# Residual-stream norms: squares summed on GpSimd, the last one by TensorE, with a later due time for that sum

## The chip, the cores and the metric

One core of one Trainium2 chip. The metric is the device time of one execution in microseconds, the median of several runs. The engines are TensorE (PE in the profile, its weight loads PEld), VectorE (DVE), ScalarE (ACT), GpSimd (POOL) and SyncE (SP), which here only issues DMAs.

## The reference, cut to what matters

Two layers over 1024 tokens of width 1024, batch 1. Each layer is a mixer (layer 0: RG-LRU and gated DeltaNet; layer 1: HGRN2 and RWKV-7), a SwiGLU feed-forward part, and a gated embedding add. Each of the three starts from a normed residual stream:

```
def _rms_norm(x, w):
    y = x * rsqrt(mean(x * x, axis=-1) + 1e-6)
    return y * w

hn = _rms_norm(h, norm_mix[layer]);  h = h + mixer(hn)
h = h + _swiglu(_rms_norm(h, norm_ffn[layer]), w_gate, w_up, w_down)
h = h + sigmoid(_rms_norm(h, norm_ple[layer]) @ ple_w_gate) * (p[layer] @ ple_w_up)
return _rms_norm(h, norm_final)
```

## The kernel before, in words

The stream is kept transposed: a half of the sequence (512 tokens) is eight tiles `h[0]` to `h[7]` of 128 channels by 512 tokens, float32. Every product with a weight matrix is made from three matmuls per 128 x 128 block, on operands split in a high and a low part (`hi*hi`, `hi*lo`, `lo*hi`): `whi`, `wlo` of the weights, `xhi`, `xlo` of the normed stream. One output tile of a width-1024 product is 24 such matmuls into one PSUM tile `acc`, of which there are four; the mixers use four others, `mx`.

The order of work is: input projection of both halves of layer 0; then four blocks, each of `project_out` (the mixer's output added to `h`), `ffn` and `ple`; behind the two blocks of layer 0 stands the input projection of layer 1 for that half (`odd_in`, through `project_in`). The mixers run beside these stages.

The norm's factor depends on the token alone, so the products are made from `h` times the norm's weight, without the factor, and the factor `rs` is multiplied in when a product leaves PSUM. `norm_scale` (from line 1154) makes `rs`. It squares the eight tiles on ScalarE (line 191 by the helper `act`) into tiles `tmp` (five buffers), adds them up pair after pair on VectorE (line 170 by `add`, seven adds), sums over the 128 channels with one float32 matmul whose weights are ones (line 196 by `mm`, into an `acc` tile; at the very first call into an `mx` tile), and then takes the inverse root: a `ts` on VectorE (line 187), Ln and Exp on ScalarE, three VectorE steps (`newton`). It is called 11 times: once for the first input projection, four times in `ffn`, four times in `ple`, twice in `odd_in`. The profile shows each float32 128x512 matmul as two instructions.

Every instruction gets a due time, `tc.cur_priority`, set by `at`; a planner with a cost model of its own plays the program through when it is built, and on each engine takes, of what is ready, the one with the smallest due time. The order it finds is then fixed. `self.clock` counts 216 for each matmul of a product (`PASS`). A product's matmuls are due at `clock`; after each output tile `products` (line 1239) sets `at(self.clock - EVAC)`, 45000 earlier, so what takes a result out of PSUM goes ahead of nearly everything. `norm_scale` is called just there: in `ffn` (line 1302) after both first tiles (gate and up, 48 matmuls) are written down, in `ple` (line 1350) after the first tile, in `project_in` (line 1271) after two tiles. Its squares, its adds, its matmul and its inverse root all carry that early due time. The splitting of weights (`weights`, line 1224) is due at `clock - WSPLIT`, 40000 ahead of its product. The mixers' instructions have due times that `spread` lays evenly over the stages beside which they run.

GpSimd is given only fills and masks: memsets and affine selects.

Of the kernel before, what the change touches and what calls it, by code (L numbers as in the profile page):

```python
# [15 lines left out]
ALU = mybir.AluOpType  # L16
# [3 lines left out]
P = 128  # L20
D = 1024
KD = D // P
# [8 lines left out]
PASS, START = 216, 100000  # L31
FETCH, WSPLIT = 28700, 40000
SPLIT, EARLY = 12000, 60000
EVAC = 45000
# [76 lines left out]
class Trunk:  # L111
# [1039 lines left out]
        for k in range(KD):  # L1151
            self.load(d[k], self.h[k])

    def norm_scale(self, acc_tile=None):

        acc = self.tmp()
        self.act(acc, self.h[0], AF.Square)
        for k in range(1, KD):
            s = self.tmp()
            self.act(s, self.h[k], AF.Square)  # L1160
            self.add(acc, acc, s)
        ps = (acc_tile or self.acc)()
        self.mm(ps, self.ones.broadcast_to([P, P]), acc)
        x = self.tmp()
        y = self.dense.tile([P, HALF], F32, tag="rs", bufs=1, name=self.name("rs"))
        self.ts(x, ps, 1.0 / D, 1e-6, ALU.mult, ALU.add)
        self.rsqrt(x, y, acc)
        return y
# [125 lines left out]
    def ffn(self, ops, wg, wu, wd, side=None):  # L1294
        starts = FSTARTS
        cols = [[self.products(w, 0, KD, P * k0, P * nk, ops) for w in (wg, wu)] for k0, nk in zip(starts, FCHUNKS)]
        rs = None

        def hidden(c):
            nonlocal rs  # L1300
            g, up = (next(p) for p in cols[c])
            if rs is None:
                rs = self.norm_scale()
            gs, t = self.tmp(), self.tmp()
            self.mul(gs, g, rs)
            self.act(t, gs, AF.Tanh, scale=0.5)
            self.stt(t, t, 1.0, gs, ALU.add, ALU.mult)
            self.mul(t, t, up)
            self.mul(t, t, rs)
            op = self.operand("g")  # L1310
            self.split(t, *op)
            return op


        ahead = []
        for c, (k0, nk) in enumerate(zip(starts, FCHUNKS)):
            hid = ahead + [hidden(c) for _ in range(nk - len(ahead))]
            ahead = [hidden(c + 1)] if c + 1 < len(FCHUNKS) else []
            for m, ps in enumerate(self.products(wd, k0, nk, 0, D, hid)):
                self.stt(self.h[m], ps, 0.5, self.h[m], ALU.mult, ALU.add)  # L1320
            if side is not None:
                next(side, None)
# [24 lines left out]
    def ple(self, ops, layer, up):  # L1347
        rs = None
        for m, g in enumerate(self.products(self.w["ple_w_gate"][layer], 0, KD, 0, D, ops)):
            if rs is None:  # L1350
                rs = self.norm_scale()
            t, u = self.tmp(), self.tmp()
            self.load(u, up[m])
            self.mul(t, g, rs)
            self.act(t, t, AF.Tanh, scale=0.5)
            self.stt(t, t, 1.0, u, ALU.add, ALU.mult)
            self.stt(self.h[m], t, 0.5, self.h[m], ALU.mult, ALU.add)
# [169 lines left out]
```

## Time and profile before

| | |
|---|---|
| median of 3 runs | 2938.49 us (2933.05 to 2941.14) |
| profiled execution, its own time | 2940.61 us |
| its span, first to last instruction | 2938.9 us |
| PE busy | 2870.5 us, 98% |
| DVE busy | 1956.7 us, 67% |
| ACT busy | 1255.6 us, 43% |
| POOL busy | 26.6 us, 1% |
| mean granted clock of TensorE | 0.99 |

How to read it: busy is the time in which an engine had an instruction of its own under way. Matmuls are pipelined: a product's matmul is shown with 0.39 us, but in a row of them one starts every 0.23 us, so what a matmul costs is read from starts, not from durations. An idle stretch is put down to whatever signalled last before the engine went on.

### The profile page before, as it was taken

The page shows a single profiled execution, that of the slowest core. Times are in us where ns is not written, and L with a number is a line of the kernel's source. Part 1 is how long each engine was busy: PE and PEld are TensorE (multiplying, and loading weights), DVE is VectorE, ACT ScalarE, POOL GpSimd, SP SyncE. Part 2 cuts the span into 40 slices and gives each one's busy share as a digit, 9 for nine tenths or more (in the row PEclk, how much of TensorE's full clock was granted, in tenths as well). Part 3 has the DMA queues.
Part 4 walks back from the last instruction along what each step waited for, and adds up shares of the span by engine and source line. Part 5 has one row for each costly group of instructions (what it writes and reads, how often), then busy time and mean ns, then how long its engine had stood idle before and what let it go on. Part 6 is the DMA issues. An engine that isn't in the chain of part 4 may idle for free.

```text
span 2938.9 us, 38745 instructions
## 1 busy us (share of the span) xinstructions
PE 2870.5 (98%) x15102; PEld 2338.9 (80%) x15102; DVE 1956.7 (67%) x3313; ACT 1255.6 (43%) x1784; POOL 26.6 (1%) x97
## 2 busy tenths in 40 slices
PE   8999999999999999999999999999999999999997
PEld 7888878878878877878877788777877777888886
DVE  7576666746686557837787674784887586655457
ACT  5354653333254636234444533533552554422234
POOL 1000000000000000000000000000000000000000
PEclk9999999999999999999999999999999999999998
DMA  6453652333345553423333544532334234343333
GB/s 207 147 171 123 215 183 89 110 83 108 87 120 175 159 180 114 107 74 100 91 106 106 162 133 146 156 97 70 101 112 109 72 111 140 96 127 93 101 89 105
DMA packets 197287, 357.79 MB, mean 122 GB/s; under 512 B 64848, under 2 KB 100816, under 8 KB 197104
## 3 DMA queue, kind: packets, MB, share of 16 engines
q1 hardware_dynamic: 197104, 355.33, 39.6%
q8 instruction: 118, 1.93, 0.3%
q14 instruction: 65, 0.53, 0.1%
HBM read 298.61 MB, written 56.66 MB: 121 GB/s over the span
## 4 chain that ended last, share of the span: by engine, by line
PE 84%; DVE 9%; ACT 3%; issue 2%; DMA 2%; SPq 0%; DVEq 0%; ACTq 0%
PE acc L196 72%; PE mx L196 11%; DVE wlo L170 2%; DVE w L183 2%; DVE w L170 1%; DVE tmp L170 1%; PE mx L207 1%; ACT w L191 1%; ACT whi L339 1%; DVE cols L170 1%; ACT L191 0%; DMA zin<-z_k 0%; DMA tmp<-mixed 0%; DVE tmp L183 0%; SPq L210 0%
## 5 line engine op out<-in xcount | busy, mean ns | idle before, releaser
L196 PE MATMUL acc<-xhi,whi 128*128 128x512 f32 x2832 | 1126.0, 398 | 14.3 <-ACT whi L339 9.1
L196 PE MATMUL acc<-xlo,whi 128*128 128x512 f32 x2832 | 1117.1, 395 | 2.2 <-DVE xlo L170 2.1
L196 PE MATMUL acc<-xhi,wlo 128*128 128x512 f32 x2832 | 1112.5, 393 | 2.8 <-DVE wlo L170 2.7
L339 ACT CAST whi<-wraw 128x1024 fp32r<-128x1024 f32 (+1 forms) x450 | 463.4, 1030 | 1142.5 <-PE acc L196 837.6
L196 PEld LDWEIGHTS acc<-xhi,whi 128*128 128x128 f32 x2832 | 532.5, 188 | 132.3 <-ACT whi L339 10.5
L196 PEld LDWEIGHTS acc<-xlo,whi 128*128 128x128 f32 x2832 | 533.2, 188 | 120.5 <-DVE xlo L170 7.6
L196 PEld LDWEIGHTS acc<-xhi,wlo 128*128 128x128 f32 x2832 | 532.8, 188 | 120.4 <-DVE wlo L170 5.7
L170 DVE TENSOR_TENSOR wlo<-wraw,whi 128x1024 fp32r<-128x1024 f32 (+1 forms) x450 | 538.6, 1197 | 77.3 <-ACT whi L339 74.8
L170 DVE TENSOR_TENSOR tmp<-acc,rs 128x512 f32<-128x512 f32 (+1 forms) x205 | 140.7, 689 | 344.4 <-PE acc L196 340.5
L196 PE MATMUL acc<-ghi,whi 128*128 128x512 f32 x736 | 290.2, 395 | 1.0 <-ACT ghi L339 1.0
L196 PE MATMUL acc<-ghi,wlo 128*128 128x512 f32 x736 | 287.6, 391 | 0.0
L196 PE MATMUL acc<-glo,whi 128*128 128x512 f32 x736 | 287.5, 391 | 0.0
L170 DVE TENSOR_TENSOR tmp<-tmp,acc 128x512 f32<-128x512 f32 x88 | 60.3, 685 | 160.3 <-PE acc L196 160.0
L191 ACT ACTIVATE w<-w 128x1024 f32<-128x1024 f32 (+2 forms) x124 | 113.3, 920 | 117.3 <-DVE w L170 52.8
L196 PEld LDWEIGHTS acc<-ghi,whi 128*128 128x128 f32 x736 | 138.0, 188 | 30.7 <-ACT ghi L339 1.9
L196 PEld LDWEIGHTS acc<-ghi,wlo 128*128 128x128 f32 x736 | 138.2, 188 | 29.2 <-issue 0.3
L196 PEld LDWEIGHTS acc<-glo,whi 128*128 128x128 f32 x736 | 138.3, 188 | 28.5 <-DVE glo L170 0.6
L183 DVE SCALAR_TENSOR_TENSOR h<-acc,h 128x512 f32<-128x512 f32 x144 | 98.5, 685 | 58.2 <-PE acc L196 57.3
L191 ACT ACT_TABLE_LOAD x85 | 109.1, 1283 | 9.6 <-DVE w L187 4.1
L183 DVE SCALAR_TENSOR_TENSOR w<-zin,cols,w 128x256 f32<-128x256 f32 x192 | 83.0, 478 | 9.7 <-ACT w L191 9.4
L191 ACT ACTIVATE tmp<-tmp 128x512 f32<-128x512 f32 x120 | 75.6, 630 | 31.7 <-DVE tmp L170 30.8
L183 DVE SCALAR_TENSOR_TENSOR tmp<-tmp,tmp 128x512 f32<-128x512 f32 x120 | 82.1, 685 | 9.6 <-ACT tmp L191 9.1
(300 smaller groups left out, 2534.2 us busy)
## 6 DMA issues: line engine op xcount, KB each, us to landing
wraw<-in_ffn_w_gate_dram SPq DMA_DIRECT2D x88, 512.0 KB, 3.6
wraw<-in_ffn_w_up_dram SPq DMA_DIRECT2D x88, 512.0 KB, 3.6
wraw<-in_ffn_w_down_dram SPq DMA_DIRECT2D x64, 512.0 KB, 3.6
wraw<-in_o_w_in_dram SPq DMA_DIRECT2D x60, 512.0 KB, 3.6
wraw<-in_e_w_in_dram SPq DMA_DIRECT2D x48, 512.0 KB, 3.7
wraw<-in_ple_w_gate_dram SPq DMA_DIRECT2D x32, 512.0 KB, 3.6
wraw<-in_ffn_w_down_dram SPq DMA_DIRECT2D x32, 384.0 KB, 3.0
up<-tmp SPq DMA_DIRECT2D x32, 256.0 KB, 2.9
```

Of the source, the lines that this page charges most:

```text
L170: (eng or self.nc.vector).tensor_tensor(out, a, b, op=op)
L183: self.nc.vector.scalar_tensor_tensor(out, a, s, b, op0=op0, op1=op1)
L191: self.nc.scalar.activation(out, a, f, **kw)
L196: self.nc.tensor.matmul(out, lhsT, rhs, start=start, stop=stop)
L207: self.nc.tensor.transpose(out, a, self.ident)
L339: self.nc.scalar.copy(hi, src)
```

## The change: what it does

In all calls of `norm_scale`, the first six of the seven adds go to GpSimd. The seventh is left out: the ones-matmul is run twice into the same PSUM tile, over the sum of the first seven squares and then over the eighth square alone.

In `ffn` and `ple`, the two ones-matmuls and what follows them in `norm_scale` get a later due time: the `clock` at which the second output tile's matmuls of that stage are due (in `ffn` that is `clock - 24 * PASS`, since the clock already stands behind two tiles). Behind `norm_scale` the due time is set back to what it was. The calls in `project_in` pass no `when` and keep the early due time.

```diff
-    def norm_scale(self, acc_tile=None):
+    def norm_scale(self, acc_tile=None, when=None):
         acc = self.tmp()
         self.act(acc, self.h[0], AF.Square)
         for k in range(1, KD):
             s = self.tmp()
             self.act(s, self.h[k], AF.Square)
-            self.add(acc, acc, s)
+            if k < KD - 1:
+                self.tt(acc, acc, s, ALU.add, self.nc.gpsimd)
         ps = (acc_tile or self.acc)()
-        self.mm(ps, self.ones.broadcast_to([P, P]), acc)
+        if when is not None:
+            self.at(when)
+        for i, t in enumerate((acc, s)):
+            self.mm(ps, self.ones.broadcast_to([P, P]), t, i == 0, i == 1)
...
             if rs is None:      # ffn
-                rs = self.norm_scale()
+                rs = self.norm_scale(when=self.clock - 24 * PASS)
+                self.at(self.clock - EVAC)
...
             if rs is None:      # ple
-                rs = self.norm_scale()
+                rs = self.norm_scale(when=self.clock)
+                self.at(self.clock - EVAC)
```

## Rows read from the trace of the kernel before

**Rows 1.** The page, part 1: busy us (share) x instructions, by engine.
```profile
PE 2870.5 (98%) x15102; PEld 2338.9 (80%) x15102; DVE 1956.7 (67%) x3313; ACT 1255.6 (43%) x1784; POOL 26.6 (1%) x97
```
**Rows 2.** The page, part 4: the chain that ended last, shares by engine.
```profile
PE 84%; DVE 9%; ACT 3%; issue 2%; DMA 2%; SPq 0%; DVEq 0%; ACTq 0%
```
**Rows 3.** Waits of PE: who waited for whom, us in total, times, longest.
```profile
PE mx L196 <- DVE keepC L183: 4.9, 4, 2.7
PE acc L196 <- DVE tmp L170: 4.7, 2, 3.7
PE mx L207 <- DVE keepB L170: 3.0, 2, 2.7
...
PE mx L196 <- DVE tmp L170: 1.4, 1, 1.4
```
**Rows 4.** Timeline of PE around the ones-matmul of the first `ffn`: start, us, instruction.
```profile
460.00 1.02 PE L196 MATMUL acc<-tmp,ones 128*128 128x512 f32 x2
460.45 0.79 PE L196 MATMUL acc<-xlo,whi 128*128 128x512 f32 x1
461.08 0.39 PE L196 MATMUL acc<-xhi,wlo 128*128 128x512 f32 x1
461.31 0.40 PE L196 MATMUL acc<-xhi,whi 128*128 128x512 f32 x1
```
**Rows 5.** Groups by line and shape: count, busy us, mean ns, idle before.
```profile
L170 DVE TENSOR_TENSOR tmp<-tmp,tmp 128x512 f32<-128x512 f32 x77 | 52.8, 685 | 2.5 <-ACT tmp L191 2.3
...
L196 PE MATMUL acc<-tmp,ones 128*128 128x512 f32 x20 | 11.5, 657 | 4.7 <-DVE tmp L170 4.7
```
**Rows 6.** Groups of POOL by line and shape.
```profile
L287 POOL TENSOR_SCALAR_AFFINE_SELECT lm<-lm 128x128 f32<-128x128 f32 x6 | 2.8, 471 | 0.3
L526 POOL MEMSET cols<- 128x512 f32 x4 | 2.1, 530 | 253.9 <-PE mx L196 240.3 <-DMA h<-in_x_dram 13.6
```
**Rows 7.** Timeline of DVE, 16.7 to 19.5 us.
```profile
16.73 0.68 DVE L170 TENSOR_TENSOR tmp<-tmp,tmp 128x512 f32<-128x512 f32 x1
...
17.52 0.78 DVE L170 TENSOR_TENSOR tmp<-tmp,tmp 128x512 f32<-128x512 f32 x1
```
**Rows 8.** Timeline of POOL, 16.7 to 19.8 us.
```profile
17.91 0.66 POOL L287 TENSOR_SCALAR_AFFINE_SELECT lm<-lm 128x128 f32<-128x128 f32 x1
...
19.40 0.34 POOL L287 TENSOR_SCALAR_AFFINE_SELECT lm<-lm 128x128 f32<-128x128 f32 x1
```
**Rows 9.** Timeline of PE at the third `ple`, 2398.8 to 2409 us.
```profile
2403.63 2.07 PE L196 MATMUL acc<-tmp,ones 128*128 128x512 f32 x2 [3.71 <-DVE tmp L170]
2404.72 1.42 PE L196 MATMUL acc<-xhi,whi 128*128 128x512 f32 x1
2408.85 0.44 PE L207 MATMUL mx<-ident,keepB 128*128 128x128 f32 x1 [2.71 <-DVE keepB L170]
```
**Rows 10.** Timeline of DVE in the same stretch.
```profile
2402.90 0.68 DVE L170 TENSOR_TENSOR tmp<-tmp,tmp 128x512 f32<-128x512 f32 x1
2403.50 1.22 DVE L170 TENSOR_TENSOR w<-keepA 128x1024 f32<-128x1024 f32 x1
2405.74 0.69 DVE L187 TENSOR_SCALAR tmp<-acc 128x512 f32<-128x512 f32 x1 [1.03 <-PE acc L196]
...
2407.48 1.22 DVE L170 TENSOR_TENSOR keepB<-keepB,w 128x1024 f32<-128x1024 f32 x1
```
**Rows 11.** Windows: us, busy (x) by engine, granted clock, DMA share, GB/s.
```profile
2402.60:2412.80 10.20, 6.45 (x19) 4.53 (x20) 9.17 (x13) 6.06 (x7) 0.00 (x0) 0.50 0.40 128
```
**Rows 12.** Timeline of PE at the fourth `ple`.
```profile
2876.86 1.12 PE L196 MATMUL acc<-tmp,ones 128*128 128x512 f32 x2 [1.00 <-DVE tmp L170]
```
**Rows 13.** Timeline of PE at the first input projection.
```profile
22.01 1.12 PE L196 MATMUL mx<-tmp,ones 128*128 128x512 f32 x2 [1.37 <-DVE tmp L170]
```
**Rows 14.** Timeline of DVE at the first `odd_in`, 919 to 940 us.
```profile
920.67 0.69 DVE L170 TENSOR_TENSOR tmp<-tmp,tmp 128x512 f32<-128x512 f32 x1
...
926.99 0.68 DVE L170 TENSOR_TENSOR tmp<-tmp,tmp 128x512 f32<-128x512 f32 x1
...
936.79 0.69 DVE L183 SCALAR_TENSOR_TENSOR rs<-tmp,rs 128x512 f32<-128x512 f32 x1
937.51 1.94 DVE L170 TENSOR_TENSOR tmp<-acc,rs 128x512 f32<-128x512 f32 x3
```

## The prediction

> **What bounds the kernel now.** I read the busy shares first. PE is busy 98% of the span, DVE 67%, POOL 1% [rows 1], and the chain that ended last lies on PE for 84% [rows 2]. So time is gained or lost where PE stands still, or where it is given more or less work. Second, the waits of PE: they are short, and many different things end them. What concerns this change is two waits for the last add of a norm, 4.7 us in `acc` sums, and one of 1.4 us in the first sum [rows 3]. That is 6.1 us on three of the eleven calls; on the other eight PE did not stand still for the sum at all. Third, the timelines around the three. They show that one of them costs more than its idle time.
>
> **The added matmul.** Each call gets a second ones-matmul. Its price is read from starts: the first of its two instructions starts at 460.00, the next product's matmuls at 460.45 and 461.08, the one after at 461.31 [rows 4]. From 460.00 to 461.08 PE did the ones-matmul and one matmul of the product; an undisturbed one takes 0.23 us (461.08 to 461.31). So 1.08 - 0.23 = 0.85 us for one ones-matmul. The 657 ns that the groups give for each of its two instructions [rows 5] are pipelined durations and would overstate it. Eleven calls: 11 x 0.85 = +9.4 us. It has no cover: PE is the bound, the operands are full-size, and only idle time just behind it could hide it, which in eight calls isn't there. At half clock one costs about twice that, so the bounds are 9.4 and 19; I take +9.4, since nearly all calls fall in stretches at full clock.
>
> **The third `ple` (2403 us).** PE waits 3.71 us for the last add, runs one sum and one product matmul, and waits 2.71 us for the mixer's `keepB` [rows 9]. In between the granted clock is 0.50, that is 1.2 GHz, for 10.2 us after the idle [rows 11], in which PE was busy 6.45 us; at full clock that would have been half. So this place loses 3.71 + 2.71 + 3.2 = 9.6 us. The cause is DVE, which has a queue without gaps here, the norm's adds in it, and then itself waits 1.03 us for the sum that PE could not start, with `keepB` behind that [rows 10]. The change takes seven adds of 0.60 us (start to start, 2402.90 to 2403.50) out of this queue, 4.2 us, and the 1.03 us as well. `keepB` then ends 5.2 us earlier, and PE goes on at 2403.6 in place of 2408.85. The sum that was already done by then comes later, 0.85 us. Net -4.4 us. What is late next is `keepB` again, so PE still stands for some 3.7 us and the clock probably still falls; if not, all 9.6 us go. On the other side, if POOL's adds hold DVE up (below), DVE is no earlier and the place is up to 3 us worse. I take -4.4, from the rows of this very place; bounds -9.6 and +3.
>
> **The fourth `ple` (2877 us).** PE waits 1.00 us for the last add [rows 12] in the middle of the stage's first tile. Planned behind that tile, some 5 us later, the sum finds its squares ready. -1.0 us; bounds -1.0 and 0.
>
> **The adds on POOL.** The trace shows no two-input instruction on POOL. The nearest rows: a fill of the same 128x512 takes 0.53 us, an affine select of a quarter of the size 0.47 us [rows 6], which scales to 1.9. I take 1.2 us, the middle, between 0.53 and 1.9. In `ffn` and `ple` the squares come 2 to 5 us apart, as the tiles of `h` do, the eighth square passes POOL by, and the sum is due a tile later: the adds are hidden there whichever bound holds. In `odd_in` they are not spread out: the seven adds on DVE start from 920.67 to 926.99 [rows 14]; six on POOL at 1.2 us take 7.2 us, about the same, at 1.9 us 11.4 us, 4 us late. The early due time stays there, so PE may wait; the planner knows some POOL price and will place the sum by it. I take +0.3 us for each of the two calls, bounds 0 and 4. In the first input projection the chain is similar, with the mask building in POOL's queue between the adds; the wait of 1.37 us [rows 13] may vanish or grow by 2. I take +0.5.
>
> **DVE's relief, and its port.** DVE loses 77 adds of 0.60 us, 46 us in all. Off the path this is worth nothing. Against it: when a POOL select ran beside an add of DVE, the add took 0.78 us in place of 0.68 [rows 7] and the select 0.66 in place of 0.34 [rows 8]. So the two engines slow each other here, and 66 adds of 1.2 us could cost DVE up to 79 us, more than it is relieved of. The Trainium skill (SBUF — State Buffer, "Who interferes with whom") says that a VectorE instruction with two SBUF inputs contends with a GpSimd instruction that reads SBUF, the later one being fully blocked. By that rule DVE gains nothing and the 2403 us place gets no better; it is the second rival, and the stretch at 17.5 us agrees with it in kind, though 0.10 us there is far from a full block.
>
> **The later due time.** `rs` itself is due some 40 us later too, so the ts, Ln, Exp and the three Newton steps now stand behind weight splits (1.2 us each) and mixer work on DVE. Before, `rs` was finished 9 to 10 us after its last add (926.99 to 936.79) and products left PSUM from 937.51 on [rows 14]. The cover is the four `acc` tiles: the sum's tile is free after the ts, so PE can fill three more tiles, 3 x 24 x 0.23 = 16 us of products and more with mixer work between, before it needs the first one back. A chain of 8 to 14 us fits. I take 0; if it took over 20 us, PE would stop in each such stage.
>
> **The sum.** +9.4 - 4.4 - 1.0 + 0.6 + 0.5 = +5.1 us. The profiled execution took 2940.61 us itself (span 2938.9 and 1.7 around it), so 2945.7 for it; it lies 2.1 us above the median of 2938.49, and for a median I forecast 2943.5 us, 0.17% slower. About 0.3% (8.8 us) is what a measurement of this kernel can tell from no change, so this counts as the same. The planner will also reorder other work, the mixers' above all, whose waits make most of PE's idle time; I put that at 0 with some 8 us either way.
>
> **The rivals.**
> *1, faster: the relief of DVE reaches further.* Then the whole 9.6 us at 2403 us go, and other waits of PE for DVE shrink: `keepC` 4.9, `keepB` 3.0 [rows 3], each of which brings a stretch at half clock like that in [rows 11]. For it: DVE is what PE waits for at most places. Against it: the adds stand only near norms, and just one of the long waits does. Price, with these 7.9 us and some 6 for the half clock behind them: 9.4 - 9.6 - 1.0 - 14 = -15 us, 2923 us. It decides if DVE's queue is what is late in the last 10 us before other waits too.
> *2, slower: POOL's adds block DVE.* Each of the 66 adds holds DVE by its own length; then 2403 us is 3 us worse, and each of the other ten calls costs PE about 1 us. 9.4 + 3 + 10 = +22, less the 1.0: about 2959 us. It decides if DVE instructions beside a POOL add are seen at 1.2 us or more above their usual time.
> *3, slower: `rs` comes too late for the PSUM tiles.* In `ffn` and `ple` the chain behind the sum exceeds 20 us, and PE stops for some 2 us in each of eight stages, with the clock falling behind it: 5 + 16 = +21, 2959 us. For it: due times of splits go ahead of it. Against it: 16 us of cover and more.
> *4, the change does not do what it says:* the planner puts the sums where they were, in the first tile. Then the 1.0 and part of the 4.4 stay lost: +9, 2947 us, still near the bound.
>
> **Chances.** Forecast, with 4 in it: 0.53; rival 1: 0.21; rival 2: 0.14; rival 3: 0.08; other reordering to the slower side: 0.04. Range for 8 in 10: 2925 to 2959, from nearly rival 1 to rivals 2 and 3; the forecast's own is 2935 to 2951. Faster by over 0.3%: 0.21. Within: 0.52. Slower by over 0.3%: 0.27, rivals 2 and 3, the rest, and a hundredth from case 4.
>
> **What would show it.** PE has 22 more matmul records (15124) and DVE 77 instructions fewer; POOL's busy time rises by 35 to 125 us. In the waits of PE, none for `tmp` at the third and fourth `ple`. The ones-matmuls lie behind the first 24 matmuls of each `ffn` and `ple`, four records in a row, 1.7 us from the first to the next product matmul but one. At the third `ple`, PE's idle is 3 to 4 us in place of 6.4. The forecast is wrong if PE's idle time as a whole (span less busy time, 68 us [rows 1]) moves by more than 8 us, or if DVE's two-input instructions get longer beside POOL's adds.

## The result, and the profile after

The changed kernel takes 2969.2 us (median of 4 runs, 2967.35 to 2970.36), the kernel before 2938.4. The ratio is 1.0107, 95% interval 1.0095 to 1.0119: slower by 1.07%. The forecast was 2943.5 us in a range of 2925 to 2959, so it missed by 26 us, and the time lies 10 us above the range. The profiled executions that are compared below took 2967.4 and 2940.6 us.

First the busy shares, part 1 of the page of the changed kernel, against [rows 1]:

```profile
PE 2884.1 (97%) x15124; PEld 2342.4 (79%) x15124; DVE 1943.1 (66%) x3236; ACT 1254.7 (42%) x1782; POOL 129.8 (4%) x163
```

The counts are as the diff has them: 22 more matmul records, 77 DVE instructions fewer, 66 more on POOL. PE is busy 13.6 us longer, but the span grew by 26.7 us (2938.9 to 2965.6): half of the loss is PE standing still. And DVE, relieved of 77 adds that were 52.8 us in [rows 5], lost only 13.6 us of busy time, so its other instructions got longer.

The waits of PE in the changed kernel (who waited for whom, us in total, times, longest), against [rows 3]:

```profile
PE acc L196 <- POOL tmp L170: 5.3, 2, 3.6
PE mx L196 <- POOL tmp L170: 5.0, 1, 5.0
...
PE acc L196 <- DVE xlo L183: 3.1, 3, 2.0
```

The waits for DVE's last add are gone, and 10.3 us of waits for POOL's are there in their place.

Where the time was lost can be read without guessing, because both kernels run the same 10704 product matmuls in almost the same order. I set the start of the n-th of them in one trace against its start in the other. The difference grows in few places:

```
place                             difference, before -> behind it    step, us
first input projection             0.7 ->  8.8                       +8.2
first ple (layer 0)                8.2 ->  9.7                       +1.4
first odd_in                       9.7 -> 19.0                       +9.3
second ple (layer 0)              17.1 -> 23.1                       +6.0
second odd_in                     23.1 -> 29.3                       +6.1
just ahead of the third ple       29.0 -> 30.4                       +1.4
third ple (layer 1)               30.4 -> 25.6                       -4.8
fourth ple (layer 1)              25.8 -> 26.8                       +1.0
each of the four ffn                                                 +0.9 to +1.0
```

The sum over everything is +26.8 us; the steps listed come to some 32. Steps of 2 to 3 us also come from the length of half-clock stretches at places where nothing changed, so a single step is good to about that. The trace of before has many of these: 60.5 us at half clock in all, where the changed kernel has 63.3, and where e9 below, which keeps the order of PE and DVE and the time of before, has 38.4.

**The three sums of the input projections.** At the first one (timeline of PE, start, us, instruction, idle before):

```profile
18.71 0.50 PE L196 MATMUL acc<-xhi,wlo 128*128 128x512 f32 x1 [1.33 <-DVE wlo L170]
...
19.98 0.40 PE L196 MATMUL acc<-xlo,whi 128*128 128x512 f32 x1
25.33 3.78 PE L196 MATMUL mx<-tmp,ones 128*128 128x512 f32 x4 [4.96 <-POOL tmp L170]
28.12 1.42 PE L196 MATMUL acc<-xhi,wlo 128*128 128x512 f32 x1
```

PE stands for 4.96 us, in place of the 1.37 of [rows 13], and before that for 1.33 us because DVE's `wlo` is late, a wait that the runs with the adds on DVE do not have here. Besides, the sum now stands behind 32 product matmuls in PE's fixed order, where it stood behind 42 before: the planner took POOL's chain of six adds to be done 10 x 0.23 = 2.3 us sooner than DVE's of seven. POOL's timeline in that stretch shows why it was not:

```profile
13.83 3.39 POOL L170 TENSOR_TENSOR tmp<-tmp,tmp 128x512 f32<-128x512 f32 x2 [8.00 <-ACT tmp L191]
...
17.67 1.56 POOL L285 TENSOR_SCALAR_AFFINE_SELECT lm<-lm 128x128 f32<-128x128 f32 x2
19.18 0.70 POOL L287 TENSOR_SCALAR_AFFINE_SELECT lm<-lm 128x128 f32<-128x128 f32 x2
19.84 2.62 POOL L170 TENSOR_TENSOR tmp<-tmp,tmp 128x512 f32<-128x512 f32 x2
...
24.01 1.26 POOL L170 TENSOR_TENSOR tmp<-tmp,tmp 128x512 f32<-128x512 f32 x1
```

The first two adds take 3.39 us together, the others 1.3 us each, and the mask building of POOL's old work is queued between the second and the third add, from 17.2 to 19.8. At the first `odd_in` there is nothing else in the queue, and it is the chain alone. PE, then POOL, then DVE in the changed kernel:

```profile
935.57 0.50 PE L196 MATMUL acc<-xlo,whi 128*128 128x512 f32 x1 [0.73 <-DVE xlo L183]
939.71 3.78 PE L196 MATMUL acc<-tmp,ones 128*128 128x512 f32 x4 [3.64 <-POOL tmp L170]
```

```profile
930.07 9.58 POOL L170 TENSOR_TENSOR tmp<-tmp,tmp 128x512 f32<-128x512 f32 x6 [58.99 <-ACT tmp L191]
```

```profile
930.62 1.52 DVE L183 SCALAR_TENSOR_TENSOR h<-tmp,h 128x512 f32<-128x512 f32 x1
932.06 0.59 DVE L183 SCALAR_TENSOR_TENSOR w<-mx,cnbe,vb 128x128 f32<-128x128 f32 x2
932.58 2.93 DVE L183 SCALAR_TENSOR_TENSOR xlo<-h,cols,xhi 128x512 fp32r<-128x512 f32 x2
936.75 1.78 DVE L183 SCALAR_TENSOR_TENSOR xlo<-h,cols,xhi 128x512 fp32r<-128x512 f32 x1 [1.24 <-ACT xhi L191]
```

Six adds take 9.58 us, 1.6 each, where DVE's seven took 7.0 between its other work [rows 14]. And DVE's `xlo`, 0.74 us before, now takes 1.2 to 1.8 us. The two small matrix instructions `w<-mx,...`, which read PSUM and one SBUF tile, keep their 0.34. After the idle comes the half clock, granted clock 0.50, the lower of TensorE's two levels (us, busy by engine, granted clock, DMA share, GB/s):

```profile
23.50:30.30 6.80, 4.97 (x8) 2.62 (x9) 2.73 (x7) 1.44 (x3) 3.02 (x10) 0.50 0.19 40
938.30:945.10 6.80, 5.39 (x9) 2.94 (x10) 0.92 (x2) 0.30 (x1) 2.98 (x6) 0.50 0.15 48
1603.90:1614.10 10.20, 10.20 (x87) 7.86 (x87) 5.80 (x7) 5.13 (x8) 2.53 (x2) 0.50 0.43 123
```

Half of PE's busy time in such a stretch is lost. So the 9.3 us of the first `odd_in` are 4.8 of idle (3.64, 0.73 and a smaller one), 5.39 / 2 = 2.7 of half clock, and 0.85 for the second sum, 8.4 in all; 0.9 us stays open. At the second `odd_in` PE does not wait for POOL at all. It waits for `xlo`:

```profile
1690.45 0.50 PE L196 MATMUL acc<-xlo,whi 128*128 128x512 f32 x1 [2.00 <-DVE xlo L183]
```

With 0.69 us for the mixer's `r_S` right behind it, the idle there is 2.7 us.

**The second `ple`.** No sum is late here; DVE, then POOL, then PE:

```profile
1597.47 3.08 DVE L183 SCALAR_TENSOR_TENSOR xlo<-h,cols,xhi 128x512 fp32r<-128x512 f32 x2
1600.48 0.68 DVE L183 SCALAR_TENSOR_TENSOR h<-acc,h 128x512 f32<-128x512 f32 x1
1601.19 1.24 DVE L621 STREAM_TRANSPOSE m<-m 32x1024 f32<-32x1024 f32 x1
```

```profile
1596.97 1.29 POOL L170 TENSOR_TENSOR tmp<-tmp,tmp 128x512 f32<-128x512 f32 x1 [236.72 <-ACT tmp L191]
1598.72 1.29 POOL L170 TENSOR_TENSOR tmp<-tmp,tmp 128x512 f32<-128x512 f32 x1 [0.46 <-ACT tmp L191]
```

```profile
1602.57 0.18 PE L196 MATMUL mx<-m,pm 32*32 32x32 f32 x1 [1.57 <-DVE m L621]
```

Two `xlo` took 3.08 us beside two POOL adds, where two take some 1.4 without. The second ended at 1600.55 us, 0.54 us behind the end of the second POOL add at 1600.01. It is so throughout: 22 `xlo` of the changed kernel began while a POOL add had more than 0.2 us still to run, and every one ended 0.55 us behind the end of that add. The two engines do not share the time, one waits for the other. The mixer's transpose behind them came 1.57 us late for PE, and the third window above, 10.2 us at half clock, followed. This is POOL's work slowing DVE, with nobody waiting for POOL.

**The added sums and the third `ple`.** Around the first `ffn`, against [rows 4]:

```profile
467.94 1.02 PE L196 MATMUL acc<-tmp,ones 128*128 128x512 f32 x2
468.40 0.79 PE L196 MATMUL acc<-xhi,wlo 128*128 128x512 f32 x1
469.02 1.02 PE L196 MATMUL acc<-tmp,ones 128*128 128x512 f32 x2
469.48 0.79 PE L196 MATMUL acc<-xhi,whi 128*128 128x512 f32 x1
```

From 467.94 to 469.02 PE did one sum and one product matmul, 1.08 us: the price of a sum is 0.85 us again. At the third `ple`, against [rows 9]:

```profile
2429.66 0.39 PE L196 MATMUL acc<-xhi,whi 128*128 128x512 f32 x1
2431.73 1.12 PE L196 MATMUL acc<-tmp,ones 128*128 128x512 f32 x2 [1.68 <-POOL tmp L170]
2432.29 0.80 PE L196 MATMUL acc<-xlo,whi 128*128 128x512 f32 x1
```

The idle is 1.68 us in place of 6.4, and at 0.39 to 0.40 us a matmul the clock did not fall. But the sum stands behind one matmul of the stage's first tile, as before, not behind the tile. And 12 us ahead of it PE waits 1.20 us for the mixer's `w` on DVE, which it did not in the trace of before: the step just ahead of the third `ple`. With it the place gains 3.3 us, not 4.8. The same two steps stand in e1, e7 and e10, three of the other runs with these POOL adds.

### The profile page after: what moved, and what is told of

The parts are those of the page before. It is cut to its first block, busy times and chain, and to the rows that moved or that the text cites. A ratio compares the mean times of both kernels' runs of the same rounds, so it can differ in the third digit from the quotient of the medians.

```text
span 2965.6 us, 38868 instructions
## 1 busy us (share of the span) xinstructions
PE 2884.1 (97%) x15124; PEld 2342.4 (79%) x15124; DVE 1943.1 (66%) x3236; ACT 1254.7 (42%) x1782; POOL 129.8 (4%) x163
## 5 line engine op out<-in xcount | busy, mean ns | idle before, releaser
L196 PE MATMUL acc<-xhi,whi 128*128 128x512 f32 x2832 | 1125.9, 398 | 14.9 <-ACT whi L339 10.3
L170 DVE TENSOR_TENSOR wlo<-wraw,whi 128x1024 fp32r<-128x1024 f32 (+1 forms) x450 | 540.1, 1200 | 83.2 <-ACT whi L339 80.6
L170 POOL TENSOR_TENSOR tmp<-tmp,tmp 128x512 f32<-128x512 f32 x66 | 103.7, 1571 | 1439.1 <-ACT tmp L191 1438.1
L183 DVE SCALAR_TENSOR_TENSOR h<-acc,h 128x512 f32<-128x512 f32 x144 | 98.5, 685 | 61.2 <-PE acc L196 60.5
```

Source lines behind the costliest of these rows:

```text
L170: (eng or self.nc.vector).tensor_tensor(out, a, b, op=op)
L183: self.nc.vector.scalar_tensor_tensor(out, a, s, b, op0=op0, op1=op1)
L196: self.nc.tensor.matmul(out, lhsT, rhs, start=start, stop=stop)
```

## The experiments

Four things could cost: waits for POOL's chain at the three sums with the early due time (A), the added sums (B), POOL's adds slowing DVE (C), and the later due time. Each run was timed beside the kernel before.

| run | median, us | ratio to before, 95% interval |
|---|---|---|
| the change | 2969.2 | 1.0107 (1.0095 to 1.0119) |
| e1, input projections as before | 2946.9 | 1.0032 (1.0021 to 1.0043) |
| e2, the adds on DVE | 2943.7 | 1.0025 (1.0016 to 1.0034) |
| e3, one sum | 2967.0 | 1.0098 (1.0082 to 1.0113) |
| e4, the due time alone | 2938.3 | 1.0005 (0.9996 to 1.0015) |
| e5, later due time in the projections too | 2962.8 | 1.0082 (1.0061 to 1.0103) |
| e6, ballast adds on POOL | 2963.2 | 1.0085 (1.0071 to 1.0099) |
| e7, only the two `ple` of layer 1 | 2934.5 | 0.9994 (0.9985 to 1.0002) |
| e8, only the input projections | 2956.6 | 1.0068 (1.0053 to 1.0082) |
| e9, fills in place of the ballast | 2936.4 | 1.0004 (0.9995 to 1.0013) |
| e10, due time and the two `ple` | 2935.8 | 0.9998 (0.9990 to 1.0007) |

**e1 and e8: which calls.** In e1 the three calls of the input projections are put back, in e8 only they are changed:

```diff
# e1, from the changed kernel
-            if k < KD - 1:
+            if when is None:
+                self.add(acc, acc, s)
+            elif k < KD - 1:
                 self.tt(acc, acc, s, ALU.add, self.nc.gpsimd)
...
+        parts = (acc,) if when is None else (acc, s)
...
# e8: the same with `when is not None`, and no later due time
```

> The three calls from the input projections (the first one and the two odd_in) are put back to seven adds on DVE and one ones-matmul; the eight calls in ffn and ple stay as changed. Theory A (the loss is PE waiting at those three early-due sums for a chain of POOL adds that the planner took to be faster than it is; matmul by matmul against before these three places are 8.2 + 9.3 + 6.1 = 23.6 us): about 2946 us. Theory B (the loss is the added ones-matmuls, 0.85 us a call): only 3 x 0.85 us go, 2967 us. Theory C (POOL's adds slow DVE at all eleven norms, about 2.8 us each): 8 us go, 2961 us.

> The converse of the first experiment: only the three calls from the input projections are changed (six adds on POOL, two ones-matmuls), ffn and ple stay as before. Theory A (the loss lies at these three places, as places, whatever happens elsewhere): before plus 22 to 24 us, 2960 us. If the loss there came from what the ffn and ple changes did to the plan ahead of them: under 2950 us.

e1 gives back 22.3 us of the 30.8, e8 alone costs 0.68%, 20 us. Together, 0.32% and 0.68%, they make 1.00% of the 1.07%. So two thirds of the loss lie at three of the eleven calls, whatever is done in `ffn` and `ple`. The 9 us that e1 keeps are the other steps of the table: in e1's own trace 6.0 at the second `ple`, 3.8 in the four `ffn`, 1.4 and 1.0 at the first and fourth `ple`, less 3.3 at the third. In e8 the waits of PE show it with the same sizes as in the change:

```profile
PE mx L196 <- POOL tmp L170: 4.9, 1, 4.9
...
PE acc L196 <- POOL tmp L170: 3.6, 1, 3.6
PE acc L196 <- DVE xlo L183: 2.7, 2, 2.0
```

The third line says that A is not all of it there: the step at the second `odd_in` begins with a wait for `xlo`, not for POOL.

**e2: the same with the adds on DVE.**

```diff
             if k < KD - 1:
-                self.tt(acc, acc, s, ALU.add, self.nc.gpsimd)
+                self.add(acc, acc, s)
```

> As changed (two ones-matmuls, later due time in ffn and ple), but the six adds are on DVE. A and C both: no wait for POOL is left; before plus 11 x 0.85 us of matmuls, less what the third ple gained (4 to 6 us): 2942 us. B alone, with POOL blameless: 2969 us stays. If the due time were the cause: 2969 us stays as well.

2943.7 us: where the adds run is worth 25 us, and what is left, 0.25% or 7 us, is near the 9.4 us of the sums less 1.5 us at the third `ple`, where PE's wait for the last add is 1.90 us with six adds in place of 3.71 with seven.

**e3: one sum.**

```diff
                 self.tt(acc, acc, s, ALU.add, self.nc.gpsimd)
+            else:
+                self.add(acc, acc, s)
...
-        for i, t in enumerate((acc, s)):
-            self.mm(ps, self.ones.broadcast_to([P, P]), t, i == 0, i == 1)
+        self.mm(ps, self.ones.broadcast_to([P, P]), acc)
```

> As changed (six adds on POOL, later due time in ffn and ple), but the seventh add is on DVE and there is one ones-matmul. B (each added ones-matmul costs PE its 0.85 us, eleven calls): 9.4 us less than the change, 2960 us, if the added DVE step behind POOL costs nothing. If that step makes PE wait 0.7 us more at the sums that are late: 2962 us. If the added matmuls lay in idle time: 2969 us.

A miss: 2967.0 us, only 2 us below the change, with intervals that overlap. Taking eleven sums away did not give 9.4 us back. Some of PE's waits in this run grew:

```profile
PE acc L196 <- DVE xlo L183: 7.4, 7, 2.2
...
PE mx L196 <- DVE tmp L170: 5.1, 1, 5.1
...
PE acc L196 <- DVE tmp L170: 3.1, 1, 3.1
```

The seventh add came back to a DVE that POOL was slowing, and `xlo` waits went from 3.1 to 7.4 us; in three of the four `ffn`, where a wait of 0.48 us for `xlo` came in, the step only fell from 1.0 to 0.7. But PE's idle as a whole grew by 1.6 us only (81.6 to 83.1). The larger part is half clock: 75.7 us in this trace, 63.3 in that of the change, of which half, 6.2 us, is lost. Why the clock fell more often here was not tested. The price of a sum stands by the first `ffn`, where the step of 0.86 us is gone in this run, and by e2, where with all adds on DVE the four `ffn` and the first `odd_in` cost 0.82 to 0.87 us each.

**e4 and e5: the due time.** e4 is the kernel before with the later due time only; e5 is the change with a later due time for the three early sums as well:

```diff
# e5, from the changed kernel, in project_in; the first call hands `when` on
-            rs = rs()
+            rs = rs(when=self.clock)
+            self.at(self.clock - EVAC)
```

> Before, with the later due time in ffn and ple alone: seven adds on DVE, one ones-matmul. If the gain at the third ple (4.8 us) and fourth ple (1 us) came from the due time: 2933 us. If it came from taking the adds off DVE: 2938 us. If the late due time costs by itself (rs too late for the PSUM tiles): 2945 us or more.

> As changed, and the three calls from the input projections get the later due time too (the clock of the third tile). A, if a later due time is enough to cover POOL's lateness: the three waits for POOL go, 2946 to 2950 us. A, if the planner places a sum by its own idea of when POOL is done whatever the due time: the waits stay, 2965 to 2969 us. B and C: 2969 us.

e4 is before to within its interval. The due time alone does next to nothing: in `ffn` it moves the sum by one to five product matmuls, for it stood within five of the start of the second tile already; in `ple` it moves the second sum by 12 and leaves the other three where they were. Why the planner left the one at the third `ple` behind one matmul is not shown. In the change, with the adds on POOL, the sums of the first, second and fourth `ple` do stand behind the whole first tile. In e5 the two waits for POOL at the first projection and first `odd_in` shrink (their steps are +2.7 and +3.6), and yet the run is 6 us better only. The second `odd_in` got worse; PE there, and the window behind it:

```profile
1679.83 0.50 PE L196 MATMUL acc<-xlo,whi 128*128 128x512 f32 x1 [2.00 <-DVE xlo L183]
```

```profile
1682.10:1695.80 13.70, 13.70 (x52) 10.14 (x50) 1.98 (x2) 2.93 (x4) 1.49 (x2) 0.50 0.25 85
```

PE waits for a slowed `xlo` and then runs 13.7 us at half clock, a step of +10.3 us. So A alone, as I had put it, fell; C had to be tested by itself.

**e6 and e9: POOL beside DVE, with nobody waiting.**

```diff
# e6, from the kernel before, in norm()
+            if 0 < k < KD - 1:
+                self.tt(self.ballast, hi[:, 0:384].bitcast(F32), hi[:, 0:384].bitcast(F32), ALU.add, self.nc.gpsimd)
# e9: a start signal, then POOL work that only writes
+            if 0 < k < KD - 1:
+                self.tt(self.ballast[:, 0:1], hi[:, 0:1].bitcast(F32), hi[:, 0:1].bitcast(F32), ALU.add, self.nc.gpsimd)
+                for _ in range(3):
+                    self.nc.gpsimd.memset(self.ballast, 0.0)
```

> Before, plus six POOL adds at each of the ten norms that make xhi and xlo from h: 128x384, float32, both inputs from the xhi tile just written, into a spare tile that nobody reads. Nothing waits for them, so only what they do to other engines shows. Theory C (a POOL add holds up DVE instructions with two SBUF inputs, xlo above all, and PE then waits for xlo or for the mixer): xlo beside them takes 1.2 us or more in place of 0.74, and the time is 5 to 15 us over before, 2942 to 2952 us. Theory A alone: 2937 us, no change.

> The control of the ballast: at the same 60 places POOL adds one column of the xhi tile (so that it starts at the same moment) and then fills the 128x384 spare tile three times, about 1.2 us of POOL that writes SBUF and hardly reads it. Theory C as a matter of two readers: xlo and the adds of DVE keep their 0.74 and 0.68 us, and the time stays at 2937 to 2940 us. If any POOL work beside DVE costs (writing, or the signals between the engines): 2955 to 2963 us, as the ballast.

e6 costs 0.85%, 25 us, over the 5 to 15 expected, although nothing waits for the ballast and DVE runs the same instructions in the same order as before. Trace against trace of e9, PE stands still 13.9 us longer (83.2 for 69.3) and has 27.5 us more at half clock (65.9 for 38.4), of which half is lost; the two together make up the 27.5 us between the spans. Groups of DVE, then of POOL (count, busy us, mean ns), in e6:

```profile
L183 DVE SCALAR_TENSOR_TENSOR h<-acc,h 128x512 f32<-128x512 f32 x144 | 98.6, 686 | 56.1 <-PE acc L196 55.4
...
L183 DVE SCALAR_TENSOR_TENSOR xlo<-h,cols,xhi 128x512 fp32r<-128x512 f32 x72 | 64.0, 925 | 5.4 <-ACT xhi L191 5.4
...
L170 DVE TENSOR_TENSOR tmp<-tmp,tmp 128x512 f32<-128x512 f32 x77 | 58.6, 761 | 2.5 <-ACT tmp L191 2.3
...
L170 POOL TENSOR_TENSOR ballast<-xhi 128x384 f32<-128x384 f32 x60 | 68.8, 1147 | 1390.0 <-ACT xhi L191 1387.5
```

and in e9:

```profile
L170 DVE TENSOR_TENSOR tmp<-tmp,tmp 128x512 f32<-128x512 f32 x77 | 52.9, 686 | 2.5 <-ACT tmp L191 2.4
L183 DVE SCALAR_TENSOR_TENSOR xlo<-h,cols,xhi 128x512 fp32r<-128x512 f32 x72 | 50.9, 745 | 5.4 <-ACT xhi L191 5.4
...
L1187 POOL MEMSET ballast<- 128x384 f32 x180 | 75.6, 420 | 10.5
```

`xlo` (two SBUF tiles read) goes from 745 to 925 ns on average, DVE's adds from 685 to 761; `h<-acc,h` (one PSUM, one SBUF tile) stays at 686. In e6 too, the 27 `xlo` that began while a ballast add had more than 0.2 us to run all ended 0.55 us behind it. With fills, more POOL time than the ballast and at the same moments, both means are as before and the kernel takes its time of before. So it is two readers of SBUF, a POOL add and a DVE instruction with two SBUF inputs, that get in each other's way, and this costs time without any wait for POOL. The Trainium skill (SBUF — State Buffer, "Who interferes with whom") says just this: such a DVE instruction contends with a GpSimd one that reads SBUF, not with one that only writes it. e6 and e9 agree with it.

**e7 and e10: what is left of the gain.** e7 changes the two `ple` calls of layer 1 alone; e10 adds the later due time in all of `ffn` and `ple`, which e4 had shown to be worth nothing.

```diff
# e7, from the kernel before; norm_scale as in e1
-                rs = self.norm_scale()
+                rs = self.norm_scale(when=self.clock if layer else None)
```

> Only the two ple calls of layer 1 are changed (POOL adds, two ones-matmuls, later due time), the nine others stay as before. The place where the change gains by its alignment with before is the third ple, 4.8 us net of its own added matmul; the fourth loses the 1 us wait and pays 0.85. If the gain stands by itself: 2932 to 2934 us, a little faster than before. If it needs the relief of DVE in the stages ahead of it: 2937 to 2939 us.

> The due time of ffn and ple as changed, one ones-matmul and seven adds on DVE everywhere, but the two ple calls of layer 1 with POOL adds and two ones-matmuls. If the gain at the third ple holds beside the due time, which itself was worth nothing: 2933 to 2935 us, at most 0.2% under before. If the due time takes the gain away: 2937 us.

In both, the step at the third `ple` is there (-4.7 us in the product matmuls' starts, -3.3 with the wait ahead of it), and so is +1.0 at the fourth. Together that is -2.3 us, near the 2.0 us that e7's median lies under the kernel before beside it; e10's lies 0.3 us under. The times are 2934.5 and 2935.8 us, and both intervals hold 1. No version is shown to beat the kernel before.

## Why the prediction was wrong

- **What bounds the kernel**: right. PE is the bound, and the losses that were found are PE idle, half clock, or more PE work.
- **The added matmul, +9.4 us**: right in its unit, 0.85 us at the first `ffn`, and steps of 0.8 to 0.9 in e2, where no add is on POOL.
- **The third `ple`, -4.4 us**: near in its number, -3.3 with the added sum and -4.2 without it. The reason, DVE's queue without the adds, holds: e4 with the adds still on DVE keeps the waits for `tmp` of 4.7 us, so it was not the due time; e2 shows that leaving out the seventh add halves the wait already. But the account was another, and that they agree is partly luck. It had PE wait some 3.7 us for `keepB` and the clock fall all the same; the wait for `keepB` went and the clock did not fall, which it had priced at up to -9.6. New waits, 1.20 us for `w` and 1.68 us for POOL's last add, took much of that back. In the trace of before this place has its half clock at 10.2 us, in e9 at 6.8, so some of the gain is chance.
- **The fourth `ple`, -1.0 us**: wrong. The wait of 1.00 us is gone, but 0.47 us for `wlo` and 0.36 us for `xlo` stand in its place, and the stage is 1.0 us longer, the added sum and 0.15 us more. In e2, with the adds on DVE, PE does not wait there.
- **The adds on POOL: the step that failed.** It took 1.2 us an add and charged +0.3 us for each `odd_in` and +0.5 for the first projection, with bounds of 4 and 2. Measured: +9.3, +6.1 and +8.2, 23.6 us, or 21.0 without the three added sums, in place of 1.1. The unit was off by a third; in the changed kernel's own group an add takes

```profile
L170 POOL TENSOR_TENSOR tmp<-tmp,tmp x66: 1260/1606/2318, 13.8 to 2901.7; 128x512 f32<-128x512 f32 x66
```

  1.26 us at least and 1.61 in the median. So the chain was longer, 9.58 us for the 7.2 at the first `odd_in`, and "the planner will place the sum by it" went the wrong way: in PE's order it put the three sums 10, 14 and 15 product matmuls earlier than before (3, 3 and 5 of them because a seventh add is missing, as e2's order shows). PE's idle at the three places is 4.9, 4.8 and 2.7 us, and the half clock behind each wait, which the prediction had charged at the third `ple` but not here, took about 2.5, 2.7 and 1.7 more. Not all of it is a late sum: the 2.7 us are waits for DVE, as are 1.3 of the 4.9 and 1.2 of the 4.8. Nor were the adds hidden in every `ple`, as was said: at the third, PE waits 1.68 us for POOL.
- **DVE's relief and its port**, taken at 0: the second failure, and the same mechanism as rival 2. The trace of before had it in one row, 0.78 us for 0.68 [rows 7], which I called far from a full block. That row could not tell: the add, from 17.52 to 18.30 us, met the last 0.32 us of a select that is not in [rows 8], so there was little to lose.

```profile
17.43 0.41 POOL L285 TENSOR_SCALAR_AFFINE_SELECT lm<-lm 128x128 f32<-128x128 f32 x1
```

  Beside whole POOL adds `xlo` takes up to 1.8 us. That makes the larger part of the 6.0 us of the second `ple` and starts the 6.1 of the second `odd_in`. Both signs by which the forecast was to be known as wrong are there: PE's idle grew from 68.3 to 81.6 us, and DVE's two-input instructions got longer.
- **The later due time**, taken at 0: right in the time, e4. Rival 3 did not happen there, and rival 4 held for the third `ple` only.
- **The chances**: rival 2, at 0.14 and 2959 us, is the nearest and had the mechanism of e6, but it left out the waits for POOL's chain. No rival had both. Its own condition, 1.2 us or more above the usual time, was set a little high: the longest `xlo` took 1.08 us more.

How much of the waits for POOL is POOL's own length and how much its slowing by DVE was not separated. An estimate for the first `odd_in`, from the shortest add: 6 x 1.26 = 7.6 us in place of 9.58, so 2 of the 3.64 us of that wait may be contention.

## What to carry to other kernels

When work is moved to an idle engine, price three things: its own duration there, what it does to its neighbour on a shared path to memory, and where the planner, which goes by a price of its own, will put the instruction that waits for it. In an order that is fixed in advance, an instruction planned too early costs the bound engine its whole lateness and the slow clock after it; one planned too late cost nothing here. A single row in which two engines overlap and both are longer than usual is worth pricing as one waiting for the other, and not by how little it happened to lose.

## What the runs showed of the hardware that was not expected

- Sixty POOL adds of 128x384 that nobody waits for slow this kernel by 0.85%; as many fills, with more POOL time, by 0.04% with an interval that holds zero.
- A DVE `xlo` that begins while a POOL add has more than 0.2 us to run ends 0.55 us behind the end of that add, in all 22 cases of the changed kernel and all 27 of e6; alone it takes 0.745 us.
- An undisturbed 128x512 float32 add takes 1.26 us on POOL and 0.685 on DVE, 1.8 times as long.
- A wait of PE of 1.6 us on DVE was followed by 10.2 us at half clock, one of 5.0 us on POOL by 6.8 us: the length of the slow stretch did not follow the length of the wait.
